# Turning row blocks of x and of a layer's result by VectorE in 32x32 squares instead of by TensorE, in a two-layer decoder trunk on one core

## The chip, the core and the metric

The kernel runs on one core of one Trainium2 chip. The core has five engines that work side by side: TensorE (PE; its weight loads stand apart in the profile as PEld), VectorE (DVE), ScalarE (ACT), GpSimd (POOL) and SyncE (SP), which here only issues transfers. The metric is the device time of one execution in microseconds (us); several runs are taken, and one further execution is recorded by the hardware profiler.

## What is computed

A trunk of two layers over one sequence of 1024 rows with 1024 features, all in float32. Cut to what matters:

```python
h = x                                              # (1, 1024, 1024)
# layer 0: gated linear recurrence (8 heads of 128)
q, f, i, g = split(h @ w_in, 4)                    # w_in (1024, 4096)
mix = recurrence(silu(q), lb + (1 - lb) * sigmoid(f), i, silu(g)) @ w_out
h = layer_norm(ALPHA * h + mix)
h = layer_norm(ALPHA * h + conv_ffn(h))            # FFN 2816, causal conv of width 3
k, v = split(h @ shared_w_kv, 2)
# layer 1: sliding-window attention (window 128, 16 query heads, 4 key heads)
mix = attention(h @ w_q, k, v, sinks, bias) @ w_out
h = layer_norm(ALPHA * h + mix)
h = layer_norm(ALPHA * h + conv_ffn(h))
```

## The kernel before

**Operands.** The features of the sequence lie on the 128 partitions for every projection: `T` holds the turned rows as [128, 2, 8, 1024], that is 8 groups of 128 features by 1024 rows, each value as a rounded high part (index 0) and a remainder (index 1). A float32 product is made of three passes (`mm3`, lines 194 to 196: high x high, high x low, low x high). `split` (line 220) makes the two parts: ScalarE casts (line 221), VectorE subtracts (`low_part`, line 169). Rows come in 8 blocks of 128.

**Turning a block.** Rows lie in memory with a row on a partition, so a block of 128 rows has to be turned before a projection can use it. `tr` (line 203) is one TensorE transposition of 128x128; `turn_block` (line 258) makes eight of them into a psax tile of PSUM and splits it into `T`. `x_block` (line 776) does the same for the first blocks of x through two psmm tiles. Feature group k of `T` holds features 128k to 128k+127, and the weights are read with `"(kc p) c -> p kc c"`: row 128k+p is on partition p at place k (w_in at line 651, shared_w_kv at 1332, w_q at 1364).

**The start.** `x_load` loads a block as one transfer of 512 KB. The order of TensorE, SyncE, ScalarE and VectorE is written out by hand here. `first_rows` (line 745) makes the first two row blocks of head 0's i and g projection and asks the generator `x_first` (line 814) for work at three places between its passes: block 1's turn, block 2's, block 3's. `lower_bounds` (line 821) is a small chain of VectorE and ScalarE operations on the 8x2 logits. Then `ig_block` (line 702) projects two row blocks at a time (tp = 1, 2, 3), 8 pairs of matmuls for each block (lines 714 and 715), and `x_pair` (line 785) puts the turns of blocks 4 and 5 beside tp = 1 and those of 6 and 7 beside tp = 2. The head's q and f projection follows.

**What sets the order.** `Order` (line 55) is a small planner: `od.t` is TensorE's planned time, `od.v` VectorE's; a generator that yields a number is taken up again that many planned us later (`od.tick` after each group of matmuls), or at the latest when `od.finish` asks for it. TensorE's order is always written out; that of the other engines is written out at the start and in the attention layer, and in the FFN it is left to the framework, which goes by priority (`urgent` raises it). SyncE's order is written out at the start only.

**Between the layers.** `Down` (line 513) makes the second FFN product in seven products of half-size blocks, in the order 1, 2, 5, 6, 7, 3, 4. Product p = 3 completes row blocks 0 to 3 and p = 4 blocks 4 to 7. `evacuate` (line 585) adds the last part, and `ln_next` (line 1314) then normalises the block (`ln_affine`, line 246), stores it in the DRAM tensor `h2d` (line 256), which later serves as residual, and returns the generator `ln_mid` (line 266), which turns the block after 11 planned us (blocks 0 to 3, so beside product p = 4) or 22 (blocks 4 to 7, so after it). After the products stand `k_part(0)` (line 1345: keys of blocks 0 to 3), `v_part(0)` and `v_part(1)` (line 1359), half a query projection, then, behind `od.finish(lns[4:6])` at line 1524, `v_part(2)`, and behind `od.finish(lns[6:])` at 1528 `k_part(1)`. The operands of a product are loaded by SyncE (lines 529 to 537) into a ring of four buffers (`rx`, `rd`), cast and subtracted into `HL`, `HT` or `T`.

The lines that the steps speak of are in the listing.

Of the kernel before, what the change touches and what calls it, by code (L numbers as in the profile page):

```python
# [13 lines left out]
AF = mybir.ActivationFunctionType  # L14
ALU = mybir.AluOpType

P = 128
# [90 lines left out]
def trunk(ctx: ExitStack, tc: tile.TileContext, a: dict, out: bass.AP):  # L108
# [48 lines left out]
    def hl_at(i):  # L157
        return HL[:, 2 * i:2 * i + 2, :]
# [44 lines left out]
    def tr(ps, src):  # L203
        nc.tensor.transpose(ps, src, ident)  # L204
        od.t += 0.109
# [64 lines left out]
    def row_tiles(tiles, g, b):  # L270
        for r, v in zip(tiles, (g, b)):
# [241 lines left out]
    class Down:  # L513
# [131 lines left out]
        def free_rows(self, j):  # L645
            return self.R[:, 0, 2 * j:2 * j + 2, :].rearrange("p a n -> p (a n)")


    x = a["x"][0]
    w_in = a["hgrn_w_in"][0]  # L650
    w_iv = w_in.rearrange("(kc p) c -> p kc c", p=P)
    hgrn_pool = tc.tile_pool(name="hp", bufs=1, reuse_waits="tile")
    with tc.tile_pool(name="t", bufs=1, reuse_waits="tile") as raws, hgrn_pool as hp:
        raw_tail(raws)
# [115 lines left out]
        with tc.tile_pool(name="ep", bufs=1, reuse_waits="tile") as ep:  # L770
            pr = ep.tile([17, P], F32, name="pr")

            def x_load(tb):
                nc.sync.dma_start(Y[:, tb, :], x[tb * P:(tb + 1) * P, :])

            def x_block(tb):
                ts = slice(tb * P, (tb + 1) * P)
                halves = [psmm() for _ in range(2)]
                for k in range(KC):
                    tr(halves[k // 4][:, k % 4 * P:(k % 4 + 1) * P], Y[:, tb, k * P:(k + 1) * P])  # L780
# [12 lines left out]
            nc.gpsimd.dma_start(pr[:16, :], a["hgrn_lb_logits"].rearrange("r (k p) -> (r k) p", p=P))  # L793
            nc.gpsimd.dma_start(pr[16:17, :], a["hgrn_gnorm_w"])
            with tc.manual_schedule(engines={EN.PE, EN.SP, EN.Activation, EN.DVE}):
                nc.scalar.activation(warm, nhalf, AF.Exp)
                x_load(0)
                raw0 = ig_load(0, 0)
                raw1 = ig_load(0, 1)
                for tb in range(1, 4):  # L800
                    x_load(tb)
                us = [ig_first(raw0)]
                lm = ep.tile([P, NH], F32, name="lm")
                le = ep.tile([P, 2, NH], F32, name="le")
# [9 lines left out]
                def x_first():  # L814
                    x_block(1)
                    yield 1.0
                    turn_block(2)
                    yield 1.2
                    turn_block(3)

                def lower_bounds():
                    yield 0.0
                    ps = psmm()
                    nc.tensor.transpose(ps[:, :17], pr, ident[:17, :17])
                    nc.vector.tensor_copy(par, ps[:, :17])
                    nc.vector.tensor_tensor(lm, par[:, 0:8], par[:, 8:16], op=ALU.max)
                    for r in range(2):
                        nc.vector.tensor_tensor(le[:, r, :], par[:, 8 * r:8 * r + 8], lm, op=ALU.subtract)
                    nc.scalar.activation(le, le, AF.Exp)
                    nc.scalar.activation(warm, nhalf, AF.Sigmoid)  # L830
# [5 lines left out]
                bounds = od.spawn(lower_bounds(), 4.9)  # L836
                ahead = x_first()
                ig_block(0, us, 0, ahead=ahead)
                od.finish([od.spawn(ahead), bounds])
# [473 lines left out]

    def ln_next(tb, down):
        ln_affine(tb, [down.free_rows(j) for j in range(2)], lambda hs: h2d[:, tb, hs])
        return ln_mid(tb)
# [5 lines left out]
    with (tc.tile_pool(name="ta", bufs=1, reuse_waits="tile") as raws,  # L1322
# [6 lines left out]
        sk, nsk = sinks[:, :16], sinks[:, 16:32]  # L1329
        nc.scalar.dma_start(sk, bass.AP(tensor=a["swa_sinks"].tensor, offset=0, ap=[[0, P], [1, 16]]))  # L1330
        wkv = a["shared_w_kv"]
        wkvv = wkv.rearrange("(kc p) c -> p kc c", p=P)
        Kl = at.tile([P, 2, S], F32R, name="Kl")
        Vt = at.tile([P, NB, 256], F32, name="Vt")
        khl, uv = [], []
        for c in range(2):
            hl = split_into(hl_at(4 + c), load(lambda r: [(r.rearrange("p (k c) -> p k c", k=KC),
                                                       wkvv[:, :, c * P:(c + 1) * P])]))
            khl.append(hl.rearrange("p h (k c) -> p h k c", k=KC))
        for u in range(2):  # L1340
            hl = split_into(hl_at(u), load(lambda r: [(r.rearrange("p (k c) -> p k c", k=4),
# [19 lines left out]
            proj_tok(uv, tp, ps)  # L1361
            nc.scalar.copy(Vt[:, 2 * tp:2 * tp + 2, :], ps.rearrange("p (a b) -> p a b", a=2))
# [284 lines left out]
```

## Time and profile before

| | us |
|---|---|
| median of 3 runs | 2131.9 (2131.87 to 2132.25) |
| the profiled execution | 2131.04 |
| its span, first to last instruction | 2129.3 |

In the span TensorE is busy 2119.9 us, VectorE 1760.9, ScalarE 926.5, GpSimd 132.5; the granted TensorE clock is 0.999.

How to read the rows shown below: times count from the start of the span. A row of the chain of waits has start, length and what the end of the execution hung on. A row of a timeline has start, length, engine, line, operation, what is written and read, count, and in brackets the idle time before it and what ended it. A row of a group has min/median/max in ns, or the busy time in us and the mean in ns of one, and behind the last bar the idle time before. A row of stretches has the stretch, its length, then the busy time and count of TensorE, weight loads, VectorE, ScalarE and GpSimd, the granted clock, the transfers' share and GB/s. A DMA's time to landing counts from its issue. `psmm` and `psax` are tiles of PSUM; in a matmul row the first name read is the streamed operand, the second the loaded weights.

### The profile page before, as it was taken

What the parts mean: (1) busy time and instruction counts of PE and PEld (TensorE: products, weight loads), DVE (VectorE), ACT (ScalarE), POOL (GpSimd) and SP (SyncE); (2) the same over time, 40 slices, a digit from 0 to 9 for tenths busy, and PEclk for the clock granted to TensorE, in tenths of its full rate; (3) what the DMA queues carried; (4) which work ended last, traced back from release to release, by engine and by line L of the source; (5) the groups of instructions that cost most, each with busy time, mean ns of one, the idle gap of its engine ahead of it and who ended that gap; (6) DMA issues with size and microseconds to landing.
All of it is one profiled execution on the core that took longest, in us unless ns stands there. A gap on an engine that the chain in (4) does not pass through costs nothing.

```text
span 2129.3 us, 32129 instructions
## 1 busy us (share of the span) xinstructions
PE 2119.9 (100%) x12663; PEld 1779.6 (84%) x12663; DVE 1760.9 (83%) x2375; ACT 926.5 (44%) x1491; POOL 132.5 (6%) x150
## 2 busy tenths in 40 slices
PE   9999999999999999999999999999999999999998
PEld 8888888888888888888888888888888888888887
DVE  4777776677999999887988658969999999978986
ACT  4444444452444444434433356743544444444430
POOL 1000000001100000000001113321000000000002
PEclk9999999999999999999999999999999999999999
DMA  5655443214223222228854411042233222249662
GB/s 216 243 211 169 144 132 119 75 32 177 99 85 98 85 89 79 80 99 275 288 190 161 129 26 45 24 149 89 80 100 98 90 86 83 86 148 325 229 215 90
DMA packets 229838, 278.96 MB, mean 131 GB/s; under 512 B 29960, under 2 KB 158648, under 8 KB 226872
## 3 DMA queue, kind: packets, MB, share of 16 engines
q1 hardware_dynamic: 228736, 276.53, 39.0%
q8 instruction: 99, 1.62, 0.3%
q10 hardware_dynamic: 856, 0.37, 0.1%
q14 instruction: 51, 0.42, 0.1%
q0 software_dynamic: 96, 0.02, 0.0%
HBM read 213.94 MB, written 62.94 MB: 130 GB/s over the span
## 4 chain that ended last, share of the span: by engine, by line
PE 99%; DMA 0%; DVE 0%; SPq 0%; issue 0%; DVEq 0%
PE psmm L194 17%; PE psmm L196 17%; PE psmm L195 17%; PE psax L194 10%; PE psax L196 10%; PE psax L195 10%; PE psmm L714 5%; PE psax L200 4%; PE psmm L715 3%; PE psmm L204 1%; PE psmm L200 1%; PE psax L204 1%; PE psax L1427 1%; PE psmm L1274 1%; DMA Y<-in_x_dram 0%; PE psmm L752 0%
## 5 line engine op out<-in xcount | busy, mean ns | idle before, releaser
L194 PE MATMUL psmm<-T,HL 128*128 128x512 f32 x768 | 303.4, 395 | 0.0
L196 PE MATMUL psmm<-T,HL 128*128 128x512 f32 x768 | 299.4, 390 | 0.0
L195 PE MATMUL psmm<-T,HL 128*128 128x512 f32 x768 | 299.2, 390 | 0.0
L473 DVE SCALAR_TENSOR_TENSOR Y<-Y,cwt 128x1023 f32<-128x1023 f32 (+1 forms) x176 | 225.0, 1281 | 44.3 <-ACT Y L471 42.9
L221 ACT CAST HL<-rx 128x1024 fp32r<-128x1024 f32 (+1 forms) x151 | 150.7, 1007 | 178.3 <-PE psmm L195 30.9
L169 DVE TENSOR_TENSOR HL<-rx,HL 128x1024 fp32r<-128x1024 f32 (+1 forms) x151 | 178.5, 1188 | 16.9 <-ACT HL L221 16.8
L714 PE MATMUL psmm<-HL,T 128*128 128x512 f32 x496 | 176.8, 399 | 0.0
L196 PEld LDWEIGHTS psmm<-T,HL 128*128 128x128 f32 x768 | 144.2, 188 | 30.7
L194 PEld LDWEIGHTS psmm<-T,HL 128*128 128x128 f32 x768 | 144.3, 188 | 29.6 <-issue 0.4
L195 PEld LDWEIGHTS psmm<-T,HL 128*128 128x128 f32 x768 | 144.3, 188 | 28.8 <-issue 0.4
L471 ACT ACTIVATE Y<-Y,cwt 128x1024 f32<-128x1024 f32 x88 | 108.7, 1238 | 101.6 <-DVE Y L460 89.4
L715 PE MATMUL psmm<-HL,T 128*128 128x256 f32 x496 | 138.9, 280 | 0.0
L194 PE MATMUL psax<-T,HL 128*128 128x512 f32 x352 | 137.3, 390 | 0.0
L196 PE MATMUL psax<-T,HL 128*128 128x512 f32 x352 | 137.0, 389 | 0.0
L195 PE MATMUL psax<-T,HL 128*128 128x512 f32 x352 | 137.0, 389 | 0.0
L243 POOL TENSOR_TENSOR rs<-rs,nhalf 128x1 f32<-128x1 f32 x32 | 44.6, 1394 | 1286.6 <-DVE rs L242 1286.6
L714 PEld LDWEIGHTS psmm<-HL,T 128*128 128x128 f32 x496 | 93.1, 188 | 21.0
L715 PEld LDWEIGHTS psmm<-HL,T 128*128 128x128 f32 x496 | 93.7, 189 | 0.4
L221 ACT CAST HT<-rx 128x1024 fp32r<-128x1024 f32 (+1 forms) x37 | 35.5, 960 | 127.9 <-DVE rx L427 76.4
L169 DVE TENSOR_TENSOR HL<-raw,HL 128x1024 fp32r<-128x1024 f32 x51 | 62.1, 1219 | 20.2 <-ACT HL L176 19.3
L195 PEld LDWEIGHTS psax<-T,HL 128*128 128x128 f32 x352 | 66.2, 188 | 13.7
L196 PEld LDWEIGHTS psax<-T,HL 128*128 128x128 f32 x352 | 66.1, 188 | 13.6
(315 smaller groups left out, 5232.3 us busy)
## 6 DMA issues: line engine op xcount, KB each, us to landing
rx<-in_ffn_w_in_dram SPq DMA_DIRECT2D x136, 256.0 KB, 3.2
rx<-gd SPq DMA_DIRECT2D x118, 256.0 KB, 3.9
Y<-in_ffn_w_out_dram SPq DMA_DIRECT2D x44, 512.0 KB, 6.4
bsd<-Y SPq DMA_DIRECT2D x22, 1024.0 KB, 4.8
gd<-Y SPq DMA_DIRECT2D x44, 512.0 KB, 2.6
rx<-in_ffn_w_out_dram SPq DMA_DIRECT2D x54, 256.0 KB, 4.7
R<-bsd SPq DMA_DIRECT2D x44, 256.0 KB, 5.1
Y<-in_ffn_w_in_dram SPq DMA_DIRECT2D x40, 256.0 KB, 2.9
```

What stands on the lines that cost most here:

```text
L169: make = lambda e: e.tensor_tensor(lo, src, hi.bitcast(F32), op=ALU.subtract)
L194: nc.tensor.matmul(ps, st(0), mv(0), start=start, stop=False)
L195: nc.tensor.matmul(ps, st(0), mv(1), start=False, stop=False)
L196: nc.tensor.matmul(ps, st(1), mv(0), start=False, stop=stop)
L200: nc.tensor.matmul(ps, lhsT, rhs, start=start, stop=stop, **kw)
L204: nc.tensor.transpose(ps, src, ident)
L221: nc.scalar.copy(hi, src)
L243: nc.gpsimd.tensor_tensor(rs, rs, nhalf, op=ALU.pow)
L471: nc.scalar.activation(c, u, AF.Identity, bias=cwt[:, l, 3, ci:ci + 1], scale=cwt[:, l, 2, ci:ci + 1])
L473: nc.vector.scalar_tensor_tensor(c[:, sh:], u[:, :S - sh], cwt[:, l, 2 - sh, ci:ci + 1], c[:, sh:], op0=ALU.mult, op1=ALU.add)
L714: nc.tensor.matmul(ps, T[:, 0, kc, ts], w[:, :, kc % 4, :], start=kc == 0, stop=False)
L715: nc.tensor.matmul(ps[:, :256], T[:, 1, kc, ts], w[:, 0, kc % 4, :], start=False, stop=kc == KC - 1)
```

## The change

Blocks 3 to 7 of x and blocks 0, 1, 2, 4, 5, 6 and 7 of the first layer's result are no longer turned by TensorE. Their rows are loaded by `quarters`: column quarter q (256 columns) of the rows goes to partitions 32q to 32q+31, with row 32b+t of the block on partition 32q+t. One VectorE instruction (`nc.vector.transpose`) then turns 32x32 squares, reading every eighth column, so that partition p of group k gets feature 8p+k. `split_turned` splits this SBUF tile into `T`. So that all of `T` has that order, the remaining TensorE turns (x blocks 0, 1, 2 and result block 3) read columns k, k+8, k+16, ..., and the weight rows are read as `"(p kc) c -> p kc c"`. x blocks 4 and 5, and 6 and 7, are loaded together, in four transfers; the result blocks are loaded back from `h2d`. The turned tiles lie in blocks of `Y` that are free by then, and for result blocks 0 to 2 in free parts of `R`. The chain on the logits is cut into two and taken into `x_first`, and the loads of the key weights become urgent.

```diff
         for kc in range(KC):
-            tr(ps[:, kc * P:(kc + 1) * P], Y[:, tb, kc * P:(kc + 1) * P])
+            tr(ps[:, kc * P:(kc + 1) * P], Y[:, tb, kc::KC])
...
-    def ln_mid(tb):
-        yield 11.0 if tb < 4 else 22.0
-        turn_block(tb)
+    def quarters(to, rows):
+        for q in range(4):
+            nc.sync.dma_start(to[q * 32:(q + 1) * 32].rearrange("p (b d) -> p b d", b=rows.shape[0] // 32),
+                              rows[:, q * 256:(q + 1) * 256].rearrange("(b t) d -> t b d", t=32))
+
+    def turn_squares(src, turned):
+        nc.vector.transpose(turned.rearrange("p (k b t) -> p b k t", k=KC, b=4),
+                            src.rearrange("p (b d k) -> p b k d", b=4, k=KC))
+        od.vec(1.1)
+
+    def split_turned(tb, turned):
+        ts = slice(tb * P, (tb + 1) * P)
+        split(T[:, 0, :, ts], T[:, 1, :, ts], turned.rearrange("p (k t) -> p k t", k=KC))
+        od.vec(1.2)
+
+    def ln_mid(tb, down):
+        if tb == 3:
+            yield 11.0
+            turn_block(tb)
+            return
+        quarters(Y[:, tb, :], h2d[:, tb, :])
+        yield 22.0 if tb > 3 else 10.0
+        turned = Y[:, tb - 4, :] if tb > 3 else down.free_turned(tb)
+        with urgent() if tb < 3 else nullcontext():
+            turn_squares(Y[:, tb, :], turned)
+            split_turned(tb, turned)
...
+        def free_turned(self, tb):
+            return self.R[:, 1, 2 * tb:2 * tb + 2, :].rearrange("p a n -> p (a n)")
...
-    w_iv = w_in.rearrange("(kc p) c -> p kc c", p=P)
+    w_iv = w_in.rearrange("(p kc) c -> p kc c", p=P)
...
+            def x_quarters(tb, n):
+                quarters(Y[:, tb:tb + n, :].rearrange("p n d -> p (n d)"), x[tb * P:(tb + n) * P, :])
+            def x_turn(tb):
+                turn_squares(Y[:, tb, :], Y[:, tb - 3, :])
+            def x_split(tb):
+                split_turned(tb, Y[:, tb - 3, :])
...
             def x_pair(tb):
-                yield 0.0
-                turn_block(tb)
-                yield 0.5
-                turn_block(tb + 1)
+                for t in (tb, tb + 1):
+                    x_split(t)
+                    if t < NB - 1:
+                        x_turn(t + 1)
+                    yield 2.0
...
-                for tb in range(1, 4):
+                for tb in range(1, 3):
                     x_load(tb)
+                x_quarters(3, 1)
+                x_quarters(4, 2)
...
                 def x_first():
                     x_block(1)
+                    x_turn(3)
+                    lower_logits()
                     yield 1.0
                     turn_block(2)
+                    nc.scalar.activation(le, le, AF.Exp)
+                    x_split(3)
+                    nc.scalar.activation(warm, nhalf, AF.Sigmoid)
                     yield 1.2
-                    turn_block(3)
+                    x_turn(4)
+                    lower_bounds()
...
-                for tb in range(4, 6):
-                    x_load(tb)
                 raws0 = {"f": qf_load(0, 1)}
-                for tb in range(6, NB):
-                    x_load(tb)
+                x_quarters(6, 2)
                 raws0["q"] = qf_load(0, 0)
...
-                    ahead = od.spawn(x_pair(2 * tp + 2), 2.0)
+                    ahead = od.spawn(x_pair(2 * tp + 2), 0.5)
...
-        wkvv = wkv.rearrange("(kc p) c -> p kc c", p=P)
+        wkvv = wkv.rearrange("(p kc) c -> p kc c", p=P)
...
-            hl = split_into(hl_at(4 + c), load(...))
+            with urgent():
+                hl = split_into(hl_at(4 + c), load(...))
...
-        wq = a["swa_w_q"][0].rearrange("(kc p) (h e) -> p kc h e", p=P, e=64)
+        wq = a["swa_w_q"][0].rearrange("(p kc) (h e) -> p kc h e", p=P, e=64)
```

`lower_logits` is the first half of the former `lower_bounds` (the transposition of the parameters by TensorE and the four VectorE operations on the logits), and `lower_bounds` what follows the exponential.

More of the change, by code (lines that the diff above doesn't have):

```diff
@@ L779, in x_block @@
                 for k in range(KC):
-                    tr(halves[k // 4][:, k % 4 * P:(k % 4 + 1) * P], Y[:, tb, k * P:(k + 1) * P])
+                    tr(halves[k // 4][:, k % 4 * P:(k % 4 + 1) * P], Y[:, tb, k::KC])
                 for i, ps in enumerate(halves):
@@ L834, in lower_bounds, with x_first @@
                     nc.vector.tensor_scalar(lbt[:, 1, :], lbt[:, 0, :], -1.0, 1.0, op0=ALU.mult, op1=ALU.add)
-                bounds = od.spawn(lower_bounds(), 4.9)
+                def x_first():
+                    x_block(1)
+                    x_turn(3)
+                    lower_logits()
+                    yield 1.0
+                    turn_block(2)
+                    nc.scalar.activation(le, le, AF.Exp)
+                    x_split(3)
+                    nc.scalar.activation(warm, nhalf, AF.Sigmoid)
+                    yield 1.2
+                    x_turn(4)
+                    lower_bounds()
                 ahead = x_first()
                 ig_block(0, us, 0, ahead=ahead)
-                od.finish([od.spawn(ahead), bounds])
-                for tb in range(4, 6):
-                    x_load(tb)
+                od.finish([od.spawn(ahead)])
                 raws0 = {"f": qf_load(0, 1)}
-                for tb in range(6, NB):
-                    x_load(tb)
+                x_quarters(6, 2)
                 raws0["q"] = qf_load(0, 0)
@@ L1315, in ln_next @@
         ln_affine(tb, [down.free_rows(j) for j in range(2)], lambda hs: h2d[:, tb, hs])
-        return ln_mid(tb)
+        return ln_mid(tb, down)
     lns = ffn(0, begun, us, rows1, lambda tb: x[tb * P:(tb + 1) * P, :],
@@ L1336, in trunk @@
         for c in range(2):
-            hl = split_into(hl_at(4 + c), load(lambda r: [(r.rearrange("p (k c) -> p k c", k=KC),
-                                                       wkvv[:, :, c * P:(c + 1) * P])]))
+            with urgent():
+                hl = split_into(hl_at(4 + c), load(lambda r: [(r.rearrange("p (k c) -> p k c", k=KC),
+                                                           wkvv[:, :, c * P:(c + 1) * P])]))
             khl.append(hl.rearrange("p h (k c) -> p h k c", k=KC))
```

11 lines of the change are left out of this document (2 added, 9 removed).

## The prediction

> **What bounds the kernel now.** I read the page's head and the shares of its chain first, then the chain of waits in the two stretches that the change touches.
>
> ```profile
> span 2129.3 us, 32129 instructions
> ...
> PE 2119.9 (100%) x12663; PEld 1779.6 (84%) x12663; DVE 1760.9 (83%) x2375; ACT 926.5 (44%) x1491; POOL 132.5 (6%) x150
> ...
> PE 99%; DMA 0%; DVE 0%; SPq 0%; issue 0%; DVEq 0%
> ```
>
> TensorE is the whole chain: 99% of what ended last is TensorE itself. So whatever leaves TensorE's queue leaves the time, as long as nothing else becomes late. The chain at the start and between the layers (start, duration, what):
>
> ```profile
> 3.29 6.81 DMA Y<-in_x_dram
> 10.24 1.06 PE psmm L204 x8
> 11.30 1.91 PE psmm L752 x16
> 13.22 0.87 PE psax L204 x8
> 15.39 0.87 PE psax L204 x8
> 19.70 0.87 PE psax L204 x8
> 28.72 0.87 PE psax L204 x8
> ...
> 1159.64 0.87 PE psax L204 x8
> 1169.80 0.87 PE psax L204 x8
> 1207.00 0.87 PE psax L204 x8
> 1215.34 0.87 PE psax L204 x8
> ```
>
> The last wait for data is that for row block 1 of x (issued 3.29, there at 10.10). From 10.24 on the chain is TensorE's, turns (L204, eight a block) included. At 13.22 it turns block 2, at 15.39 block 3, from 19.70 to 28.72 blocks 4 to 7 (four rows, first and last shown); from 1159.64 to 1169.80 blocks 0 to 3 of the layer's result (four, first and last), from 1207.00 to 1215.34 blocks 4 to 7 (likewise). A turn is 0.87 us, 0.109 us for each transposition.
>
> **What the change removes.** Five turns at the start (3 to 7) and seven between the layers (all but 3): 12 x 0.87 = 10.4 us of TensorE, 4.35 and 6.1. All of it is on the path. What is late next decides how much is kept.
>
> **What it adds, in prices.** VectorE gets one 32x32 transposition of 128x1024 for each of the twelve blocks; casts and low parts (L221, L169) stay as many and read SBUF instead of PSUM. No row shows a transposition on VectorE. The nearest:
>
> ```profile
> L1001 DVE TENSOR_TENSOR St<-qs,kp x8: 1217/1220/1221, 62.1 to 432.4; 128x1024 f32<-128x1024 f32 x8
> L1010 DVE TENSOR_TENSOR kd<-kp,qp x16: 682/685/689, 67.1 to 437.9; 128x512 f32<-128x512 f32 x16
> L221 ACT CAST HL<-rx 128x1024 fp32r<-128x1024 f32 x135 | 141.0, 1052 | 152.1 <-PE psmm L195 27.5 <-PE psax L195 21.9 <-PE psax L196 21.2
> ```
>
> 1024 contiguous elements take 1.22 us; 512 elements whose first source steps by 16 bytes (L1010 reads every fourth float) take 0.685, on the same line of about 1.045 ns an element. The squares step by 32 bytes. Bounds: 1.2 us (this pace) to 2.44 (half of it; no row shows that step). I take 1.2, the pace of both rows. The cast from SBUF is 1.05 us.
>
> The four turns that stay on TensorE (x blocks 0 to 2, result block 3) now load weights with a step of 32 bytes.
>
> ```profile
> L204 PEld LDWEIGHTS psax<-ident,Y x64: 138/140/142, 1159.2 to 1215.8; 128*128 128x128 f32 x64
>   DMA Y<-in_x_dram: 0.5, 1
> L752 PEld LDWEIGHTS psmm<-HL,T x48: 186/189/192, 6.8 to 16.8; 128*128 128x128 f32 x48
> ```
>
> Their load takes 0.140 us now. Bounds: no change, up to twice the whole 0.140 with nothing overlapped, +0.17 us each. L752's loads of 0.189 go through at 1.91/16 = 0.119 us a pair, so I take that, +0.010. Block 0 lies ahead of the wait for block 1's rows, in which TensorE idled 0.5 us (second row); the other 24 transpositions cost 0.2 us (bounds 0 and 4.1).
>
> [...]
>
> **The start, step by step.** VectorE's and ScalarE's order is written out here, so a late step delays all behind it.
>
> ```profile
> L774 SPq DMA_DIRECT2D Y<-in_x_dram x8: 351/432/4556, 0.7 to 11.9; - x8
> DMA to landing us min/median/max: 7.0/7.2/7.4
> GB/s 0 0 0 0 154 287 266 358 326 312 319 320 330 334 338 346 339 333 347 355 342 361 389 359 399 410 430 399 451 399 420 430 366 371 348 364 384 397 443 402
> 11.52 1.29 DVE L169 TENSOR_TENSOR T<-psmm,T 128x512 fp32r<-128x512 f32 x2 [1.55 <-ACT T L221]
> 14.13 1.01 ACT L221 CAST T<-psax 128x1024 fp32r<-128x1024 f32 x1 [2.15 <-PE psax L204]
> 15.17 1.23 DVE L169 TENSOR_TENSOR T<-psax,T 128x1024 fp32r<-128x1024 f32 x1 [2.36 <-ACT T L221]
> 16.31 0.17 DVE L825 COPY par<-psmm 128x17 f32<-128x17 f32 x1
> 16.72 0.24 DVE L828 TENSOR_TENSOR le<-par,lm 128x8 f32<-128x8 f32 x2
> 17.06 0.40 PE L714 MATMUL psmm<-HL,T 128*128 128x512 f32 x1
> 19.18 0.40 PE L714 MATMUL psmm<-HL,T 128*128 128x512 f32 x1
> ```
>
> *Transfers.* The queue is full until about 20 us; it moves 320 to 346 GB/s where 512-byte pieces of w_in pass, and up to 430 where the 4 KB rows of x do (40 slices of 0.4 us). Quarters have 1 KB pieces, so they run between: five blocks are 2.62 MB, 6.1 us at 430 or 8.2 at 320, at most 2 us later for the last block. SyncE's seven issues more, 0.43 us each, run ahead of the queue. Block 3, the third issue from 3.29 on, landed near 3.29 + 2 x 0.43 + 7.2 = 11.4; as quarters I put it at 12.
>
> *VectorE.* Block 1's low parts end at 12.8 (11.52 + 1.29). The squares of block 3 run to 14.0, the logits (16.31 to 16.96 in the rows, 0.65) to 14.65. TensorE turns block 2 at 13.2 (as now), the cast ends at 15.14, its low part at 16.4, as in the rows; without block 3's turn TensorE wants it at about 16.2 (17.06 less 0.87): **0.2 us lost**. ScalarE's exponential and block 3's cast end at 16.45, its low part at 17.7, block 4's squares at 18.9, the four small operations of the bounds at 19.6, its cast at 19.95, its low part at 21.2. From there the cycle of a block on VectorE is squares 1.2, wait for the cast 1.05 (the values' small operations fill it), low part 1.23: 3.5 us. TensorE takes (19.18 - 17.06)/6 x 8 = 2.83 us a block. Blocks 4 to 7 get their low parts at about 21.2, 24.6, 28.05 and 31.5; TensorE comes at 22.05, 24.9, 27.7 and 30.9: nothing lost on 4 and 5, then 0.3 and 0.5. Losses sum to 1.0 us, and the start gains 4.35 - 1.0 = **3.35**. Past block 7 the chain ends: the weights of the first projection take two operations and are due 2.8 us later.
>
> **Between the layers.** Blocks 0 to 2 go while the last down product runs.
>
> ```profile
> 1147.40:1176.00 28.60, 28.60 (x144) 24.02 (x144) 27.27 (x34) 9.97 (x10) 5.43 (x4) 1.00 0.36 130
> 1174.22 1.22 DVE L169 TENSOR_TENSOR HL<-rx,HL 128x1024 fp32r<-128x1024 f32 x1
> 1182.09 0.39 PE L194 MATMUL psmm<-HL 128*128 128x512 f32 x1
> L256 SPq DMA_DIRECT2D h2d<-Y x8: 319/330/339, 1152.3 to 1201.5; - x8
> DMA to landing us min/median/max: 2.6/2.8/3.0
> 1201.50 0.34 SPq L256 DMA_DIRECT2D h2d<-Y  x1
> 1228.17 0.59 ACT L1362 COPY Vt<-psmm 128x512 f32<-128x512 f32 x1 [10.42 <-PE psmm L196]
> ```
>
> In the first row (length, then TensorE, weight loads, VectorE, ScalarE) VectorE is busy 27.27 of 28.60 us. The low part of the product's last operand is done at 1175.44, TensorE first uses it at 1182.09: 6.65 us of cover. Three turns less bring TensorE there 2.6 us earlier, three squares bring VectorE 3.6 us later: 0.4 us is left. Behind that stands a new wait: the squares need the reload, which needs the store's landing: 2.8 us, four issues of 0.33, some 3 us again, 7 us a block. SyncE meanwhile holds the operand loads behind it, VectorE whatever stands behind the squares. Bounds: nothing, and 3 x 7 us. Low parts of operands and the next block's norm can run in between (27.27 us of other work in those 28.6), so I stay near the lower end: 0.6 us lost.
>
> Blocks 4 to 7 are in no hurry: the store of 7 is issued at 1201.50, its reload is there by about 1209, squares, cast and low part take 3.5 us; the projection that reads blocks 4 and 5 first ended at 1228.17 and is 48 matmuls, at 0.119 some 6 us, so it wants them from 1222, or 1218.6 without the four turns. The squares stand in the turns' old places, 1207 to 1215, and 1215 + 3.5 = 1218.5 even for block 7, which is read after that projection. These 3.5 us are kept whole.
>
> *Weight rows 8p+k.* As many pieces of 512 bytes from other rows; the loads run a slot ahead. Only the first two stand before block 1 (10.24); I take no change.
>
> **Sum.** 10.4 - 1.0 - 0.6 - 0.2 = 8.6 us. The profiled execution took 2131.04 (span 2129.3 and 1.7 around it): 2122.4. The runs' median is 2131.9, 0.86 above it: **2123.3**.
>
> **Rivals.**
> - *Squares at half pace* (2.44 us). The start's cycle becomes 2.4 + 1.05 + 1.2 = 4.7 against 2.83 us of TensorE: block 2 loses 0.9, block 4 0.4, blocks 5 to 7 about 1.9 each, 6.9 in sum, so the start loses 2.5 instead of gaining; between the layers 7.2 us more on VectorE meet 4.0 of cover, 3.2 lost. Gain 10.4 - 6.9 - 3.2 = 0.3: 2131.6. Chance 0.14. [...]
> - *Strided weights at twice the load.* 4.1 us instead of 0.2: 2127.2. Chance 0.08. For it is that the load reads one float of every 32 bytes; against it, that 0.189 us loads already hide at 0.119.
> - *Quarters at half the rate.* If 32 partitions at a time take 215 GB/s, half of 430, a block takes 2.4 us instead of 1.2: block 3 is 1.2 later, blocks 6 and 7 6 us, about 25; both come just as VectorE wants them: 1 to 2 us lost, 2125. Chance 0.12. No row here has such a transfer. [...]
> - *The reload stops VectorE between the layers* (the other side). If the squares stand in VectorE's queue directly behind each norm, it waits the full 7 us three times, 21 us, while operands are due; TensorE loses all beyond the 0.4 us of cover. From 9.2 us of waiting on there is no gain, at 21 it is 2131.9 + 12 = 2144. For it: 95% busy VectorE. Against: operations ready to run in between. Chance 0.08 slower; 0.08 more for a part of it, 2125.5 to 2131.
>
> **Chances.** A measurement tells 0.2%, 4.3 us, from no change. The forecast (2121 to 2125.5) has 0.50. Faster (up to 2127.6): 0.50 + strided weights 0.06 + quarters 0.12 + part of the stop 0.04 = 0.72. Within: half pace 0.14, the rest of strided and of the stop 0.06, so 0.20. Slower 0.08. The range runs from 2121.0 (10.4 kept, and the 0.5 idle) to 2131.0, which takes in the second and third rival, a half-pace case in which a little is filled in, and most of a partial stop.
>
> **What would show it.** Right: 96 fewer L204 transpositions from Y; new VectorE operations of about 1.2 us; the first qf matmul some 3.4 us earlier; no gap in TensorE beyond 1 us in the last down product. Wrong: squares of 2 us or more, L204 blocks over 1 us, VectorE waiting for a reload with a TensorE gap behind it, or x landing after its squares' turn.

## The result, and the profile after

The changed kernel takes 2140.79 us (median of 5 runs, 2139.67 to 2144.07) against 2131.87 for the kernel before on the same chip: a ratio of 1.0047, 95% interval 1.0036 to 1.0058. It is 8.9 us slower; the forecast was 8.6 us faster.

The page of the changed kernel, its head and the shares of its chain:

```profile
span 2139.0 us, 32021 instructions
...
PE 2116.9 (99%) x12567; PEld 1772.0 (83%) x12567; DVE 1784.2 (83%) x2387; ACT 926.7 (43%) x1491; POOL 134.0 (6%) x150
...
PE 94%; DVE 3%; DMA 1%; issue 1%; ACT 1%; POOL 0%; SPq 0%; DVEq 0%; ACTq 0%; POOLq 0%
```

The 96 transpositions have gone (12663 before, 12567 now), and the span grew by 9.7 us all the same. TensorE was 99% of the chain and is 94% of it; VectorE, which was none, is 3%. Where the time came in is read from three marks on TensorE, the same matmuls in both kernels: the first of head 0's q and f projection, the first of the keys, the first of the attention scores. First the timeline of before, then that of after:

```profile
37.55 0.40 PE L194 MATMUL psmm<-T,HL 128*128 128x512 f32 x1
...
1190.93 0.39 PE L194 MATMUL psmm<-T,HL 128*128 128x512 f32 x1
...
1244.32 1.10 PE L1427 MATMUL psax<-Kh,q 128*128 128x128 f32 x8
```
```profile
40.25 0.39 PE L194 MATMUL psmm<-T,HL 128*128 128x512 f32 x1
...
1196.97 0.39 PE L194 MATMUL psmm<-T,HL 128*128 128x512 f32 x1
...
1254.21 1.10 PE L1470 MATMUL psax<-Kh,q 128*128 128x128 f32 x8
```

The start loses 2.7 us, the way to the keys another 3.3 (6.04 - 2.70), the way from there to the scores another 3.9 (9.89 - 6.04). Since turns of 4.35, 2.6 and 3.5 us were taken out of these stretches, some 7, 6 and 7 us of new stops and slow work stand in them.

The new operation, grouped by its line, with what it waited for and who waited for it (times in ns, then us):

```profile
L274 DVE STREAM_TRANSPOSE Y<-Y x9: 1998/2180/2224, 13.9 to 1230.8; 128x1024 f32<-128x1024 f32 x9
L274 DVE STREAM_TRANSPOSE R<-Y x3: 2085/2128/2151, 1166.5 to 1180.0; 128x1024 f32<-128x1024 f32 x3
its engine sat idle before it (us, times) until:
  DMA Y<-in_x_dram: 1.1, 1
who waited for it (us, times):
  ACT T L221: 22.2, 7
```

A block's squares take 2.13 to 2.18 us, not 1.2. They hardly wait for data themselves; ScalarE's casts wait for them.

VectorE in the last down product and in the second half of the keys (timeline; the bracket is the idle time before, and what ended it):

```profile
1175.62 2.13 DVE L274 STREAM_TRANSPOSE R<-Y 128x1024 f32<-128x1024 f32 x1
...
1180.01 2.08 DVE L274 STREAM_TRANSPOSE R<-Y 128x1024 f32<-128x1024 f32 x1
1183.21 1.23 DVE L169 TENSOR_TENSOR T<-R,T 128x1024 fp32r<-128x1024 f32 x1 [1.11 <-ACT T L221]
1184.35 2.36 DVE L169 TENSOR_TENSOR HL<-rx,HL 128x1024 fp32r<-128x1024 f32 x2
...
1212.70 1.39 DVE L1398 TENSOR_TENSOR Kl<-psmm,Kh 64x512 fp32r<-64x512 f32 x2 [3.36 <-ACT Kh L1396]
...
1217.65 2.15 DVE L274 STREAM_TRANSPOSE Y<-Y 128x1024 f32<-128x1024 f32 x1
...
1233.95 1.23 DVE L169 TENSOR_TENSOR T<-Y,T 128x1024 fp32r<-128x1024 f32 x1 [1.11 <-ACT T L221]
```

Squares, an idle 1.1 us for the cast, low part: 4.4 us a block, in series. The last operands' low parts (HL<-rx), due on TensorE at 1181, begin at 1184.35, behind blocks 1 and 2. ScalarE does the same one step earlier: its cast of these operands stands behind block 2's cast, which waited 3.29 us for the squares. These are ScalarE's rows and the matmul that waited:

```profile
1182.13 1.04 ACT L221 CAST T<-R 128x1024 fp32r<-128x1024 f32 x1 [3.29 <-DVE R L274]
1183.08 1.99 ACT L221 CAST HL<-rx 128x1024 fp32r<-128x1024 f32 x2
1184.17 0.50 PE L194 MATMUL psmm<-HL 128*128 128x512 f32 x1 [2.59 <-ACT HL L221]
```

Of TensorE's stop the cast makes 2.59 us, and the low parts 0.95 and 0.17 behind it. The operands are loaded late too: SyncE issues three of their four halves from 1172.58 to 1175.5, behind eight issues of reloads and a store, where the kernel before issued all four from 1162.74 to 1167.2. By the 5.4 us to landing that the trace has for one of them, the last is there between 1179 and 1181 (an estimate). No run takes this apart from the order on ScalarE and VectorE.

Block 4's squares stand behind the keys' own work, at 1217.65 instead of 1207, and block 7's low part begins at 1233.95; the forecast had it done by 1218.5.

What TensorE makes of it, by stretches of the changed kernel (length, then busy time and count of TensorE, weight loads, VectorE, ScalarE and GpSimd, the granted clock, the transfers' share and GB/s):

```profile
1181.00:1184.00 3.00, 0.58 (x3) 0.16 (x1) 1.89 (x2) 1.87 (x2) 0.00 (x0) 1.00 0.51 176
1184.00:1187.00 3.00, 1.71 (x5) 0.91 (x6) 2.71 (x3) 2.96 (x4) 0.00 (x0) 0.91 0.00 0
1187.00:1190.00 3.00, 3.00 (x8) 2.33 (x9) 1.88 (x5) 0.00 (x0) 0.00 (x0) 0.52 0.00 0
1190.00:1193.00 3.00, 3.00 (x15) 2.45 (x14) 2.34 (x3) 0.00 (x0) 1.45 (x1) 1.00 0.00 0
...
1230.00:1234.00 4.00, 0.78 (x8) 0.57 (x6) 2.89 (x3) 1.28 (x3) 0.00 (x0) 1.00 0.00 0
1234.00:1237.00 3.00, 2.31 (x5) 1.64 (x6) 2.55 (x3) 1.48 (x3) 0.00 (x0) 0.54 0.00 0
1237.00:1240.00 3.00, 3.00 (x8) 2.31 (x8) 0.00 (x0) 0.00 (x0) 0.00 (x0) 0.50 0.00 0
1240.00:1243.00 3.00, 3.00 (x12) 2.37 (x11) 0.00 (x0) 0.00 (x0) 0.00 (x0) 0.82 0.00 0
```

TensorE all but stands from 1181.6 to 1184.2 and from 1230.5 to 1234, and then comes a second loss that a count of waits doesn't show: it is busy for the whole of 1187 to 1190, yet does 8 matmuls instead of 15, at a granted clock of 0.52. The page's clock line rounds this away.

The last view is that of the transfers, 6 to 24 us in 40 slices, before and then after:

```profile
GB/s 360 321 355 335 343 358 383 364 410 419 410 419 428 419 391 398 366 357 362 402 426 404 417 428 391 323 346 352 367 357 351 350 276 122 76 57 9 0 0 0
```
```profile
GB/s 335 389 353 377 332 365 401 316 248 287 203 212 246 239 269 225 212 205 203 282 223 221 198 197 220 224 327 332 327 196 190 201 213 221 250 237 212 203 199 220
```

As soon as quarters run, the queue moves 200 to 250 GB/s in most slices, where in the kernel before it moved 320 to 430.

### The profile page after: what moved, and what is told of

The parts are those of the page before. It is cut to its first block, busy times and chain, and to the rows that moved or that the text cites. A ratio compares the mean times of both kernels' runs of the same rounds, so it can differ in the third digit from the quotient of the medians.

```text
span 2139.0 us, 32021 instructions
## 1 busy us (share of the span) xinstructions
PE 2116.9 (99%) x12567; PEld 1772.0 (83%) x12567; DVE 1784.2 (83%) x2387; ACT 926.7 (43%) x1491; POOL 134.0 (6%) x150
## 4 chain that ended last, share of the span: by engine, by line
PE 94%; DVE 3%; DMA 1%; issue 1%; ACT 1%; POOL 0%; SPq 0%; DVEq 0%; ACTq 0%; POOLq 0%
PE psmm L194 16%; PE psmm L195 16%; PE psmm L196 16%; PE psax L194 9%; PE psax L196 9%; PE psax L195 9%; PE psmm L743 5%; PE psax L200 4%; PE psmm L744 3%; PE psmm L204 1%; PE psmm L200 1%; PE psax L1470 1%; PE psmm L1316 1%; PE psax L204 1%; DVE Y L274 1%
## 5 line engine op out<-in xcount | busy, mean ns | idle before, releaser
L743 PEld LDWEIGHTS psmm<-HL,T 128*128 128x128 f32 x496 | 93.1, 188 | 23.5 <-ACT T L221 2.7
L196 PEld LDWEIGHTS psax<-T,HL 128*128 128x128 f32 x352 | 66.1, 188 | 13.8
L195 PEld LDWEIGHTS psax<-T,HL 128*128 128x128 f32 x352 | 66.1, 188 | 13.5
L194 PEld LDWEIGHTS psax<-T,HL 128*128 128x128 f32 x352 | 66.1, 188 | 13.5
```

What stands on the lines that cost most here:

```text
L194: nc.tensor.matmul(ps, st(0), mv(0), start=start, stop=False)
L195: nc.tensor.matmul(ps, st(0), mv(1), start=False, stop=False)
L196: nc.tensor.matmul(ps, st(1), mv(0), start=False, stop=stop)
L743: nc.tensor.matmul(ps, T[:, 0, kc, ts], w[:, :, kc % 4, :], start=kc == 0, stop=False)
```

## Experiments

The theory to be tested: the squares' price (2.15 instead of 1.2 us) caused the loss, because they read with a step of 32 bytes. The rivals: the transfers at half their rate, the strided weight loads, the reload between the layers. Four runs take these apart first.

**Neighbouring columns in the squares.**

```diff
-                            src.rearrange("p (b d k) -> p b k d", b=4, k=KC))
+                            src.rearrange("p (b k d) -> p b k d", b=4, k=KC))
```

> The changed kernel with one difference: the squares read 32 neighbouring columns instead of every eighth (so the features of twelve blocks stand in another order than the weight rows; the result is that of permuted features, the work is the same). Theory A: the squares cost 2.15 us because their source steps by 32 bytes. Then they fall to about 1.2 us, the waits of TensorE at the start and between the layers go, and the kernel takes 2123 to 2127 us. Theory B: a transposition of 4-byte words takes two cycles an element whatever the step. Then they stay at 2.1 to 2.2 us and the kernel at 2140 to 2142 us.

Measured: 2128.36 us, ratio 0.9985 (0.9976 to 0.9995). The squares, grouped:

```profile
L274 DVE STREAM_TRANSPOSE Y<-Y x9: 1235/1240/1245, 14.7 to 1223.0; 128x1024 f32<-128x1024 f32 x9
...
  DMA Y<-in_x_dram: 3.4, 3
```

So the step costs 0.94 us a block and, through what hangs on it, some 12 us of time. But the 8.6 us of the forecast don't come back, only some 3: the squares now wait 3.4 us for late rows of x, and the cast's wait is still there. TensorE stops for low parts at the start, 3.0 us in five stops, and for the operands' cast and low parts in the last down product, 2.0 us in three. No kernel whose weight rows follow this order of features was run.

**One half at a time.** First the start alone is changed, with all result blocks turned by TensorE (`turn_block` in `ln_mid`); then the layers alone, with the start of before.

> The changed kernel with all eight blocks between the layers turned by TensorE again (reading every eighth column); the start stays changed. If the cost of the start is what the changed kernel's trace shows there (the q and f projection begins 2.5 us later than before), this takes 2131.9 + 2.5 = 2134.4 us. If the loss between the layers came from the start's shift or from the weight rows, it would stay near 2138 to 2141.

> The kernel before with the weight rows as 8p+k, TensorE's turns reading every eighth column and the change between the layers; the start is turned by TensorE. By the trace (8.9 us in all, 2.5 of them at the start) this takes 2131.9 + 6.4 = 2138.3 us, with TensorE waiting about 6 us near the end of the last down product and 7 us before the second half of the keys. If reloads were at fault, VectorE would be seen waiting for them.

Measured: 2134.58 (ratio 1.0018, 1.0009 to 1.0028) and 2138.09 (1.0033, 1.0020 to 1.0046). Both halves lose: 3.4 and 6.9 us above the kernel before on that chip (2131.19), 10.3 together against 8.9 for the whole. The start's loss differs between executions. The first of head 0's q and f matmuls comes at 40.25 in the changed kernel's trace, but at 41.65 to 42.64 in the four other traces with the same start (start alone, the two fillers, without raised priority); block 3's squares waited 1.1 us for their rows in the former and 2.1 to 2.5 in the latter.

**Weight rows 8p+k alone**, every turn left on TensorE.

> The kernel before with the weight rows as 8p+k and all 16 turns by TensorE reading every eighth column; no squares. If weight loads with a step of 32 bytes cost nothing that matters and the transfers of w_in stay hidden: 2131.9 within 0.7 us. If the strided load took twice its time, 120 transpositions on the path would add up to 20 us; if the weight transfers got slower, the wait for x block 1 at 10.24 would move.

Measured: 2131.99 (2131.19 before on that chip), ratio 1.0004 (0.9994 to 1.0013). The psax turns' weight loads do grow:

```profile
L204 PEld LDWEIGHTS psax<-ident,Y x112: 185/193/208, 13.3 to 1216.8; 128*128 128x128 f32 x112
```

0.193 us instead of 0.140, and hidden, as the forecast had it. That rival falls.

**Where the price of the step begins.** The squares of x read with a step of 16 bytes (s = 4), those between the layers with 8 (s = 2).

```diff
-                            src.rearrange("p (b d k) -> p b k d", b=4, k=KC))
+                            src.rearrange("p (m d i) -> p m i d", i=s, d=32))
```

> The squares' source step alone is changed, from 32 bytes to 16 for the blocks of x and to 8 for the blocks between the layers; features come out permuted, so the output is not the reference's. [...] Theory M (16 bytes is still free, as the 0.685 us of L1010 suggested): both 1.24 us, time near 2128.4.

Measured: 2131.43 (1.0000, 0.9990 to 1.0010), and the two steps in one view:

```profile
L274 DVE STREAM_TRANSPOSE Y<-Y x9: 1236/2019/2058, 15.6 to 1227.0; 128x1024 f32<-128x1024 f32 x9
L274 DVE STREAM_TRANSPOSE R<-Y x3: 1235/1236/1237, 1167.4 to 1180.0; 128x1024 f32<-128x1024 f32 x3
```

The median of the first row (five blocks of x, four of the result) is that of x: 2.02 us at 16 bytes; the three blocks of the second row take 1.236 at 8 bytes. So here a step of 8 bytes costs nothing against one of 4 (1.236 against 1.240 us), and one of 16 costs 0.78 us a block: Theory M falls. L1010, the row on which the forecast leaned, takes 0.685 us for its 512 elements at a step of 16 bytes, but reads each of them twice; whether that is why it shows no cost, no run tests.

**The cast covered.** On top of neighbouring columns, the next block's squares stand between a block's cast and its low part:

```diff
-                    x_split(t)
+                    nc.scalar.copy(T[:, 0, :, ts], turned)
                     if t < NB - 1:
                         x_turn(t + 1)
+                    low_part(T[:, 1, :, ts], turned, T[:, 0, :, ts], None)
```

> Edit on top of the kernel with contiguous squares (permuted features, output not the reference's): for blocks 4 to 7 of x the next block's squares stand between a block's cast and its low part, so that VectorE no longer waits 0.8 to 1.1 us for ScalarE's cast. Theory W (the wait for the cast is what makes the start's cycle 3.5 us against TensorE's 2.83): the cycle falls to about 2.8, TensorE's stops of 1.26 us at 30 and 34 us go, time 2126.3 to 2127.5. Theory X (the late rows of x set the squares): the order changes nothing, 2128.4 within 0.6, the squares wait for x instead.

Measured: 2130.15 (0.9997, 0.9988 to 1.0006). Theory W fails: nothing is won, because the squares of block 6 now stand ahead of block 5's low part and wait for their rows:

```profile
28.06 1.25 DVE L274 STREAM_TRANSPOSE Y<-Y 128x1024 f32<-128x1024 f32 x1 [3.02 <-DMA Y<-in_x_dram]
```

**Why x is late.** Three kernels send the same 1 KB pieces in another way. The first sends 32 rows to all 128 partitions in one transfer, the second quarter q to partitions q, q+4, ..., the third quarters 2 and 3 by ScalarE's queue.

```diff
-        for q in range(4):
-            nc.sync.dma_start(to[q * 32:(q + 1) * 32].rearrange("p (b d) -> p b d", b=rows.shape[0] // 32),
-                              rows[:, q * 256:(q + 1) * 256].rearrange("(b t) d -> t b d", t=32))
+        for b in range(rows.shape[0] // 32):
+            nc.sync.dma_start(to[:, b * 256:(b + 1) * 256],
+                              rows[b * 32:(b + 1) * 32].rearrange("t (q d) -> q t d", q=4))
...
+            nc.sync.dma_start(to[q::4].rearrange("p (b d) -> p b d", b=rows.shape[0] // 32),
...
+            (nc.sync if q < 2 else nc.scalar).dma_start(
```

> Edit on top of the kernel with contiguous squares (2128.4 us, TensorE then waited for late squares of x, whose source landed at 14.7 and 20.3 us): each quarter transfer of 32 partitions x (rows of a block) becomes one transfer of 128 partitions x 1 KB for 32 rows, so pieces and bytes stay and only the span of partitions of one transfer grows; the features stay in the permuted order of that kernel, so the output is not the reference's. Theory P (the half rate comes from a destination of only 32 partitions): the stretch of 12 to 24 us moves 330 GB/s or more instead of 200 to 250, block 3 lands near 12 and block 4 near 15, VectorE's waits for x at the start (3.4 us) go, time 2126 to 2127.3. Theory Q (the rate comes from the 1 KB pieces): 200 to 250 GB/s as before, time 2128.4 within 0.6.

> On top of the kernel with contiguous squares and the cast covered (2130.2 us): quarter q goes to every fourth partition (q, q+4, ..., q+124) instead of 32 neighbours. Pieces, bytes, number of transfers and partitions of a transfer stay, only their spread changes; the values land on other partitions, so the output is not the reference's. [...] Theory Q (the 1 KB pieces set the rate): 200 to 250 GB/s, 2130.2 within 0.8.

> On top of the kernel with contiguous squares and the cast covered (2130.2 us, permuted features, output not the reference's): x's quarters 2 and 3 are issued by ScalarE, so that transfers to partitions 64 to 127 run beside those to 0 to 63. Theory R (the two halves of the partitions are served side by side once two queues feed them): 320 GB/s or more while quarters run, VectorE's waits for x fall from 5.8 to below 3 us, 2127 to 2128.5. Theory S (the 16 engines take the transfers one after the other whatever the queue): 200 to 250 GB/s, 2130 or slower, since the quarters on the second queue also come ahead of rows and weights that are due sooner.

Measured: 2157.39 (1.0122, 1.0108 to 1.0136), 2133.07 (1.0010, 1.0001 to 1.0019) and 2135.51 (1.0018, 1.0009 to 1.0027). The transfers of the first from 6 to 36 us, then those of the second from 6 to 24:

```profile
DMA  9999633222232222222224993222222222222259
GB/s 338 355 388 410 246 130 109 93 98 97 94 120 97 94 98 96 96 98 93 98 97 141 311 310 118 98 94 87 87 97 97 94 98 96 96 97 96 97 181 319
```
```profile
GB/s 330 396 377 395 394 440 411 353 385 369 373 385 385 385 364 378 363 347 353 321 150 94 3 0 0 0 0 0 0 0 0 0 0 0 210 298 349 275 32 36
```

The first decides nothing on its question: the rate is 87 to 98 GB/s in most slices and the 16 engines are busy two tenths of the time, as if 3 to 5 of them worked (an estimate from that share), and the outermost dimension of its source is 4; it met a limit that was not foreseen, and whether that dimension is the reason wasn't tested. The second decides it: with pieces, bytes, count and number of partitions unchanged and only their spread over the partitions widened, the rate goes from 200 to 250 GB/s up to 320 and more (to 15 us), and the rows of blocks 3 to 5 are there by 16 us (those of 6 and 7 are issued only at 24.3). So between these two kernels the rate hangs on which 32 partitions a transfer fills, not on the 1 KB; why it does, no run shows. The time of this kernel says nothing on the gain, since the turn of block 1 on TensorE then waited 10.2 us for transfers into the same tile. In the third the rate is 148 to 292 GB/s from 11.4 to 23.5 us, while both queues run: the second queue doesn't help here. Its quarters come ahead of rows that are due sooner.

**The last four blocks.** Only result blocks 4 to 7 go in squares (step 32 bytes), due as in the changed kernel, and then earlier:

```diff
-        if tb == 3:
+        if tb < 4:
...
-        yield 22.0 if tb > 3 else 10.0
+        yield 14.0        # second kernel only
```

> The kernel before with weight rows 8p+k, in which only result blocks 4 to 7 are turned by squares (still with the 32-byte step), blocks 0 to 3 and all of x by TensorE. Four turns, 3.5 us of TensorE, go. Theory D (blocks 4 to 7 came late because the squares of blocks 0 to 2 held up VectorE in the down product): the stop of 3.5 us before the second half of the keys goes, time 2128.4 to 2129.5. Theory E (they are late by themselves: four cycles of 4.4 us in series, begun behind the keys' own VectorE work because they are due after 22 planned us): the stop at about 1230 stays, 3 us or more, and the clock falls after it; 2132 to 2135.

> As the kernel with only result blocks 4 to 7 in squares, but these are due after 14 planned us instead of 22. Theory E: block 4's squares move ahead of the keys' VectorE work, to about 1207, the four end by 1225, no stop before the keys' second half, time 2128.4 to 2129.5. Theory F (the rows reloaded from DRAM come too late for an earlier place): VectorE then waits for a reload, and the keys' own work behind it with it; no gain over due 22.

Measured: 2132.39 (1.0003, 0.9994 to 1.0011) and 2135.26 (1.0019, 1.0011 to 1.0028). The first kernel's stretches:

```profile
1224.00:1228.00 4.00, 1.74 (x10) 1.22 (x9) 2.54 (x3) 2.61 (x4) 0.00 (x0) 0.93 0.00 0
1228.00:1231.00 3.00, 3.00 (x8) 2.32 (x8) 1.34 (x2) 0.00 (x0) 0.00 (x0) 0.52 0.00 0
```

The stop is there without any squares in the down product, though shorter (2.3 us of these 4.0), so Theory D is at most a part. The earlier due time makes it worse, and not by Theory F: no VectorE wait for a reload shows. Blocks 4 and 5 came between the keys' two VectorE steps, and the low part of the query weights, due on TensorE at 1213, moved to 1217.65 behind them.

**The same operations in a written order**, block 4's squares ahead of the keys' work, block 5's between its halves, and each further block's between the cast and the low part of the one before:

```diff
+            squares(4)
             k_part(0)                 # squares(5) behind its first half of columns
             hl = q_unit(0)
             make_lows()
+            turned_parts(4)()
+            low = turned_parts(5)     # the cast; low() is the low part
+            squares(6)
+            low()
             v_part(0)
+            low = turned_parts(6)
+            squares(7)
+            low()
             v_part(1)
+            turned_parts(7)()
```

> As the kernel with only result blocks 4 to 7 in squares (2132.4 us, correct output, TensorE stopped for 3.6 us before the keys' second half), with the same operations in another order on VectorE and ScalarE: block 4's squares ahead of the keys' own work (VectorE idled 3.4 us there), block 5's between the keys' two halves of columns, and each further block's squares between the cast and the low part of the block before. Theory E (blocks 4 to 7 were late by their place and by the wait for the cast in each cycle, not by the squares' 2.13 us or the reload): the four end near 1220, TensorE doesn't stop, 3.5 us are kept: 2127.8 to 2129. Theory G (VectorE's sum of work, or the reload of blocks 6 and 7, is too long for the stretch whatever the order): a stop of 2 us or more remains at 1213 to 1227, 2131 or more.

Measured: 2128.19 us, ratio 0.9986 (0.9977 to 0.9995), faster than both kernels. VectorE's timeline:

```profile
1200.40 2.13 DVE L274 STREAM_TRANSPOSE Y<-Y 128x1024 f32<-128x1024 f32 x1
...
1217.59 2.15 DVE L274 STREAM_TRANSPOSE Y<-Y 128x1024 f32<-128x1024 f32 x1
1219.66 2.42 DVE L169 TENSOR_TENSOR T<-Y,T 128x1024 fp32r<-128x1024 f32 x2
```

No idle time stands at a low part, the four blocks are done at 1222.1, and TensorE doesn't stop. Theory E holds, G falls: even at 2.15 us the squares fit here. What was wrong in this stretch was the order.

**Filling the stop.** On the changed kernel, matmuls without use in TensorE's queue ahead of the keys' second half:

```diff
             od.finish(lns[6:])
+            busy = psmm()
+            for _ in range(26):       # 13 in the second kernel
+                nc.tensor.matmul(busy[:, :P], ident, ident, start=True, stop=True)
             k_part(1)
```

> The changed kernel with 26 matmuls of 128x128 without use put in TensorE's queue behind the last values' projection, ahead of the keys' second half, where TensorE stopped for 3.5 us; they take about 2.9 us of that stop and delay nothing. Theory C (TensorE's clock is halved for some 6 us because it stood still for about 3 us): the granted clock stays near 1.0 from 1234 to 1243, where it was 0.50 to 0.82, and about 2.5 us come back: 2138.3, from 2140.8. Theory H (the half pace has another cause, such as VectorE's and ScalarE's traffic or late operands): the pace stays as it was, 2140.8 or a little more.

> The changed kernel with 13 matmuls of 128x128 (26 passes, 0.11 us each, 2.9 us) in the stop of 3.5 us before the keys' second half, half of the filler that took 5.7 us. Theory C (the stop itself halves the clock): granted clock 1.00 from 1234 to 1243, 2.5 us come back, 2138.3. Theory H (the half pace doesn't matter for the end, or what follows is late anyway): 2140.8 within 0.8.

Measured: 2141.44 (1.0043, 1.0029 to 1.0057) and 2139.93 (1.0038, 1.0026 to 1.0051). Each of these products is two instructions, so that the 26 took 5.97 us, longer than the stop. The 13 fit; their stretches, and the rows around them in the timeline:

```profile
1237.00:1240.00 3.00, 1.93 (x7) 1.38 (x8) 2.33 (x3) 1.82 (x4) 0.00 (x0) 1.00 0.00 0
1240.00:1243.00 3.00, 3.00 (x15) 2.47 (x14) 0.27 (x1) 0.00 (x0) 0.00 (x0) 1.00 0.00 0
```
```profile
1233.74 0.28 PE L196 MATMUL psmm<-HL,T 128*128 128x256 f32 x1
1233.87 3.06 PE L1574 MATMUL psmm<-ident 128*128 128x128 f32 x26
1237.31 0.50 PE L194 MATMUL psmm<-T,HL 128*128 128x512 f32 x1 [0.38 <-ACT T L221]
...
1254.84 1.10 PE L1470 MATMUL psax<-Kh,q 128*128 128x128 f32 x8
```

The operands come no earlier, but the clock stays at 1.00, and behind the stop 3 us hold 15 matmuls at once. From the last matmul ahead of the stop to the scores it takes 21.10 us (1254.84 - 1233.74); in the changed kernel it took 23.74 (1254.21 - 1230.47, the last value matmul there). The stretch gives back 2.6 us, as Theory C said. In the whole time only 0.9 shows, with intervals that overlap, so the total of that gain isn't settled. In the trace the stop itself comes 3.3 us later than in the changed kernel's (1233.74 against 1230.47), and 2.4 of them were lost at the start, whose code is the same.

**Blocks 0 to 2 without raised priority** (`urgent()` taken from `ln_mid`).

> The changed kernel without the raised priority of the squares, casts and low parts of result blocks 0 to 2. Theory O (their place ahead of the last operands' low parts stops TensorE at 1181): the stop of 3 us and the slow stretch behind it go, some 5 us, about 2136; the squares come later. Theory U (VectorE has more work than time in that stretch, so any order stops TensorE somewhere): the stop moves, to other operands or to the keys' first half, and the time stays within 1.5 us of 2140.8.

Measured: 2142.74 (1.0051, 1.0038 to 1.0064). The stop stays:

```profile
1184.63 1.23 DVE L169 TENSOR_TENSOR T<-R,T 128x1024 fp32r<-128x1024 f32 x1 [1.11 <-ACT T L221]
1185.77 2.35 DVE L169 TENSOR_TENSOR HL<-rx,HL 128x1024 fp32r<-128x1024 f32 x2
```

The order on VectorE is the same without it, operands' low parts last, and so is ScalarE's, with the operands' cast behind block 2's. Priority isn't the cause. Whether a written order would help in the down product as it did among the keys wasn't tried.

## Why the prediction was wrong, point by point

- **TensorE as the bound, 10.4 us removed.** Right: 96 transpositions gone, and where the squares are on time (the written order) 2.8 of 3.5 us are kept.
- **The price of the squares: the step that failed.** "I take 1.2, the pace of both rows." They take 2.13 to 2.18; at 1.24, with neighbouring columns, the kernel is some 12 us faster. The upper end of the bounds (2.44) stood in the text; the row chosen against it, L1010, reads every element twice. The price alone doesn't close the gap: at 1.24 the time is 2128.36, not 2123.3, and the next four points hold what else was missed.
- **The start at that price.** The rival with half pace worked it out: a loss of 2.5 us. Measured 2.7 in the changed kernel's trace, but 4.1 to 5.1 in the four others with the same start, so that the fit is in part luck. The cycle was forecast at 4.7 us there and is 4.45 (squares begin at 23.47 and 27.92). "The values' small operations fill" the cast's wait is wrong: 0.4 to 1.4 us of it stay idle.
- **Quarters.** "Between 320 and 430" is wrong; 200 to 250 is the rival's half rate. Behind slow squares all but block 3's rows (1.1 to 2.5 us of waits) is covered; with fast ones it is the next bound (3.4 us of waits, 5.8 with the cast covered).
- **The last down product.** Forecast 0.6 us lost, 3.2 in the rival. Lost are 5.9 (2.6 of turns gone and 3.3 later): a block costs VectorE 4.4 us in series with the cast, which neither the forecast nor the rival counted here, and the clock of 0.52 comes on top.
- **Blocks 4 to 7 "kept whole".** Wrong, and so was the rival, which took this over: 3.5 us of gain became 3.9 of loss. The squares didn't stand in the turns' places; VectorE's order put them behind the keys' work, 10 us later.
- **Strided weights, weight rows.** Right: 2131.99 with them alone, 0.8 above the kernel before on that chip and within the interval.
- **The reload stops VectorE.** Refuted as named: no wait for a reload shows on VectorE between the layers. But the forecast's other remark, that SyncE holds the operand loads behind the reload, came true: three halves are issued 6.7 to 9.5 us later than before, 2.7 of these from the start. What that costs is open.

The rival with half pace stated the cause and missed the size, 2131.6 against 2140.8: its start fits the one trace, its 3.2 us between the layers were 13 (5.9 and 7.4).

## What to carry to other kernels

Before an operation moves to another engine, price it by a row with the same access pattern, each element read once and with the same step; where no row has it, let the upper end decide what else is checked. Count the chain of a block (squares, cast, low part) in series unless the order on the engine puts other work between: the same four blocks lost 3.9 us in one order and kept 2.8 in another. A stop of TensorE is read together with the stretch behind it, since the clock there can be lower: it was 0.50 to 0.52 here.

## What the runs showed of the hardware

**The clock after a stop.** In the changed kernel TensorE worked at half its pace after each of its two stops of about 3 us between the layers: the granted clock was 0.52 from 1187 to 1190 and 0.50 from 1237 to 1240; the second cost 2.6 us by the run with 13 fillers. Stretches of half a microsecond tell how long. The clock is 0.97 in the one from 1186.0, 0.50 in those that follow and 0.61 in the one from 1189.5. If it was either 1.00 or 0.50 throughout, it fell at 1186.47 and rose at 1189.89 (an estimate from these shares). The second time, by 0.76 in the one from 1234.0 and 0.91 in the one from 1241.0, it fell at 1234.26 and rose at 1241.09. That is 3.42 and 6.83 us. The other kernels' stretches give nearly the same lengths in the same way: 3.44 with the last four blocks (0.93 over 4 us, 0.52 over 3), 3.42 and 6.84 with the layers alone (0.58 and 0.85, then 0.55, 0.50 and 0.81, each over 3 us), 6.84 without raised priority, after the stop in the last down product (0.70, 0.50 and 0.66, each over 3 us). In the kernel with the last four blocks 0.52 followed on 4.0 us in which TensorE was busy for 1.74. Not every stop does it: in the kernel with the start alone changed, TensorE does nothing in two whole microseconds and goes on at a clock of 1.00:

```profile
18.00:20.00 2.00, 0.00 (x0) 0.00 (x0) 1.91 (x6) 1.12 (x2) 0.00 (x0) 1.00 1.16 239
20.00:22.00 2.00, 1.97 (x11) 1.76 (x12) 1.94 (x2) 1.97 (x5) 0.00 (x0) 1.00 1.12 194
```

What sets these lengths, why one stop lowers the clock and another doesn't, and how much work keeps it up, no run here tests.

**Steps, quarters, spread.** A 128x1024 transposition in squares took 1.24 us at steps of 4 and 8 bytes, 2.02 at 16 and 2.18 at 32 (medians). While transfers to 32 neighbouring partitions ran, the queue moved 200 to 250 GB/s in most slices of the changed kernel; with transfers to every fourth partition it moved 320 to 440 from 6 to 15 us. The one arrangement whose source has 4 as its outermost dimension moved 87 to 98 in most slices.
